# The input's sums of squares by accumulating DMAs, with more warm-up products and a later load of the gates' weights

## The chip, the cores and the metric

The kernel runs on one core of a Trainium2 chip. The metric is the device time of one execution in microseconds (us). Five engines work beside each other, each through its own instructions in order: TensorE (PE, matrix products; PEld is its load of the stationary operand), VectorE (DVE), ScalarE (ACT), GpSimd (POOL) and SyncE (SP, which only issues DMAs here). DMAs are issued by SyncE, ScalarE and GpSimd; those that add to what stands at their target are all issued by GpSimd.

## What is computed

One residual block of a streaming encoder on `x` of 512 tokens by 2048 channels, in float32. The part around the change is its beginning:

```python
hn = rmsnorm(h, norm_mix_g)          # y = x * rsqrt(mean(x*x) + EPS) * g
proj = hn @ w_in + b_in              # 2048 x 11272
(q, k, v, o_pre, i_pre, f_pre, cb, cc, ch, gm_pre, gc_pre) = jnp.split(proj, offs, axis=-1)
```

Behind it come the mLSTM, a short convolution, their merge through gates, `w_out` with the residual, and the feed-forward part with `w_up` and `w_down`, each with products of the same kind. The factor `rsqrt(mean(x*x) + EPS)` of a token is the same for all output channels, so the kernel multiplies by it (`rstd`) after the products.

## The kernel before

Everything is kept transposed: channels on the partitions, the 512 tokens along the free axis. Products of two 256-channel blocks with the tokens are done by a scheme with seven products in place of eight (`PRODUCTS` and `P1`), and each float32 product as three passes with a high and a low part (`three`, L280 to L282: high times high, high times low, low times high).

*Cells and items.* A pair of 128-channel blocks of the activations is a cell. The input has eight (0 to 7). An item is a pair of output blocks. Its weights come in four steps for the input phase; one step holds two half steps (`r` = 0, 1), each with one cell, of 21 products (`cell_mm`). Items 0 and 1 are interleaved in steps 0 to 7; from step 8 on (`START = 8`) each item has four steps in a row: item 2 has steps 8 to 11, item 3 steps 12 to 15. Steps `2q` and `2q + 1` of the first eight use cells `2q` and `2q + 1`.

*What a cell needs* (`x_task`): a load (cells 0 to 4 into `buf`, one of `mA`, `mB`, `z2`, `zs[0]`, `zs[1]`; cells 5 to 7 into a `raw` tile), a scaling by the norm's weight on ScalarE (`scaled`, L962), sums on VectorE (L343 to L353), a high part on ScalarE (`hi`, L357), a low part on VectorE (`lo`, L360), and a square on ScalarE (L952) for the sum over channels. For cells 0 to 4 the square follows `hi` and overwrites `buf`; for cells 5 to 7 it stands ahead of the scaling and goes from `raw` into `xbufs[c % 5]`, that is `mA`, `mB`, `z2`.

*What a step's weights need* (`weight_task`): a load into one of six `raw` tiles; sums on VectorE (L212 to L222); per half a high part on ScalarE (L232, four buffers) and a low part on VectorE (L236, three buffers). The load is SyncE's DMAs (L251 and L252 fill 128 KB each, L261 brings 512 KB), and GpSimd's two accumulating DMAs of 128 KB into the fills (L254). Steps 0, 1, 2 and 4 (`ALONE`) load 512 KB alone and do the first sum on VectorE.

*Sums of squares* (`sum_tokens`): eight products with `ones` per cell (L442) into bank `SIDE`, one output column each. In steps 0, 2, 4 and 6 one such group follows each half step. `rows_stages` makes `rstd` of it: `cols_a` (scale, square root), `cols_b` (reciprocal, correction, and L453, a diagonal of the result), `rows_pe` (L456, the product of `ones` with the diagonal) and `rows_post` (a copy to `rstd`).

*Order of the beginning.* `order` lists the tasks: cell 0, step 0's weights, cell 1, step 1's weights, and so on to cell 7, step 7's weights, then step 8's and on. The loop from L1242 on goes through it: in iteration `i` it emits the sums and high part of task `i + 1` (with the scaling of task `i + 2` between them), the low part of task `i`, the loads that have become possible (six tasks ahead of the last finished low part), and the half steps that have all their operands. Ahead of it come 18 warm-up products on zeros (L1195), `pcol`'s first part, the first loads, and the load of the gates' weights `gst` into `mC` on ScalarE's queue (L1207; eight of 264 columns of `w_v0`, so 32 bytes at a time).

Behind the loop stand `small_loads` (ten small DMAs on GpSimd), the weights of steps 8 and 9, and the main loop over the steps. A step `s` of it emits, in this order: VectorE's work for the weights of steps `s + 1` and `s + 2`, interleaved with the evacuations of items that ended (L310 to L313); `side_posts`; TensorE's two half steps; `gate_step`; one entry of `side`, whose first function is emitted at once, and whose second becomes a side post of the next step; and from step `START + hold` on the posts of ended items (L688, the multiplication by `rstd`, and more), of which items 0 and 1 have been waiting since step 8. So `cols_a` is emitted in step 8, `cols_b` and the product of `rows_pe` in step 9, `rows_post` in step 10.

*The gates.* `gate_weights`, in step 8, clears a `raw` tile on GpSimd (L478) and fills it from `gst` on ScalarE and VectorE (L482 to L485). `gate_mm` (L498 to L503) follows the half steps of step 9 (cells 0 to 2), step 10 (3 to 5) and step 11 (6 and 7); the result is copied from its bank in step 11.

Of the kernel before, what the change touches and what calls it, by code (L numbers as in the profile page):

```python
# [12 lines left out]
ALU = mybir.AluOpType  # L13

P = 128
T = 512
# [4 lines left out]
DV = 256  # L21
# [23 lines left out]
def kpair(c):  # L45

    q, r = divmod(c, 2)
    return 4 * q + r, 4 * q + 2 + r
# [23 lines left out]
def tile_block(ctx: ExitStack, tc: tile.TileContext, xT, w1, w_v0, w_v1, w_v2, w_bm, w_bc, w_out, w_up, w_down,  # L72
               par, b_if, b_v, outT):
    nc = tc.nc
    V, A, G, PE, SP = nc.vector, nc.scalar, nc.gpsimd, nc.tensor, nc.sync
# [14 lines left out]
    def f(ap):  # L90
        return ap.bitcast(F32)

    def C(shape, dt, s):
        return const.tile(shape, dt, tag=s, name=s)
# [15 lines left out]
    rstd = C([P, T], F32, "rstd")  # L110

    def col(base, j): return pcol[:, base + j:base + j + 1]
    def g_mix(j): return col(0, j)
# [9 lines left out]
    P_BANK, SIDE = bank[3], bank[7]  # L123
    SETS = (bank[0:3], bank[4:7])

    mA, mB, mC = C([P, 1280], F32, "mA"), C([P, 1032], F32, "mB"), C([P, T], F32, "mC")
    z2 = C([P, 2 * T], F32, "z2")
    zs = [C([P, 2 * T], F32, f"z{i}") for i in range(2)]
# [12 lines left out]
    side, posts, side_posts, late = deque(), deque(), [], []  # L141
# [275 lines left out]
    def rsqrt_a(src, scale, eps, n):  # L417

        v, y = sm("nv")[:, :n], sm("ny")[:, :n]
        if isinstance(eps, float):  # L420
            V.tensor_scalar(v, src, scale, eps, op0=ALU.mult, op1=ALU.add)
        else:
            V.scalar_tensor_tensor(v, src, scale, eps, op0=ALU.mult, op1=ALU.add)
        A.activation(y, v, AF.Sqrt)

    def rsqrt_b(dst, n):

        v, y, t = sm("nv")[:, :n], sm("ny")[:, :n], sm("nt")[:, :n]
        V.reciprocal(y, y)
        V.tensor_mul(t, y, y)  # L430
        V.tensor_mul(t, t, v)
        V.tensor_scalar(t, t, -0.5, 1.5, op0=ALU.mult, op1=ALU.add)
        V.tensor_mul(dst, y, t)
# [3 lines left out]
    def sum_tokens(ps, sq, n, nt, first, last):  # L437

        for b in range(n):
            for t in range(nt):  # L440
                o = (b * nt + t) * P
                PE.matmul(ps[:, t:t + 1], sq[:, o:o + P], ones[:, 0:1], start=first and b + t == 0,  # L442
                          stop=last and b == n - 1, skip_group_check=True)

    def rows_stages(ps, dst, diag, nt=4):

        def cols_a():
            rsqrt_a(ps[:, :nt], 1.0 / D, EPS, nt)

        def cols_b():  # L450
            rsqrt_b(rs1[:, :nt], nt)
            for t in range(nt):
                V.tensor_scalar(diag[:, t * P:(t + 1) * P], ident, rs1[:, t:t + 1], None, op0=ALU.mult)  # L453

        def rows_pe():
            PE.matmul(SIDE[:, :nt * P], ones, diag[:, :nt * P], start=True, stop=True)  # L456

        def rows_post():
            A.activation(dst[:, :nt * P], SIDE[:, :nt * P], AF.Copy)  # L459

        return cols_a, cols_b, rows_pe, rows_post
# [7 lines left out]
    gb = [mA[:, :T], mA[:, T:2 * T], mB[:, :T], mB[:, T:2 * T], mC, z2[:, :T], z2[:, T:]]  # L469

    gst = mC[:, :KD * 8].rearrange("p (k n) -> p k n", n=8)
# [455 lines left out]
            j1, j2 = kpair(p)  # L927
            x_items.append(Item(tiles_load(w1, c + j1, c + j2), 4, X, sig_post(d, c, j1, j2, s)))

    sqs = {}  # L930
    xbufs = [mA, mB, z2, zs[0], zs[1]]

    def x_task(c):

        k1, k2 = kpair(c)
        t = cell_task(X, c, xT)
        cell_load = t.load
        buf = xbufs[c % 5]

        def load():  # L940
            if c < 5:
                SP.dma_start(buf[:, :T], xT[k1])
                SP.dma_start(buf[:, T:2 * T], xT[k2])
            else:
                cell_load()

        def square(srcs):
            assert c < 5 or c - 5 not in sqs
            sqs[c] = buf
            for i, src in enumerate(srcs):  # L950
                w = src.shape[-1]
                A.activation(buf[:, i * w:(i + 1) * w], src, AF.Square)  # L952

        def scaled():
            if c < 5:
                t.new_raw()
                srcs = buf[:, :T], buf[:, T:2 * T]
            else:
                srcs = t.two()
                square(srcs)  # L960
            for ap, src, k in zip(t.two(), srcs, (k1, k2)):
                A.activation(ap, src, AF.Copy, scale=g_mix(k))  # L962

        cell_hi = t.hi

        def hi():
            cell_hi()
            if c < 5:
                square([buf[:, :2 * T]])

        t.load, t.pre, t.hi = load, scaled, hi
        return t
# [115 lines left out]
    order = [t for ts in tasks for t in ts]  # L1088
# [4 lines left out]
    def load_next():  # L1093
        i = n_load[0]
        while n_lo[0] < i and order[n_lo[0]].done:
            n_lo[0] += 1
        if i == len(order) or i - n_lo[0] + held[0] == RAW or (order[i].ready and not order[i].ready()):
            return False
        order[i].load()
        n_load[0] += 1  # L1100
        return True

    def loads():
        while load_next():
            pass
# [5 lines left out]
    def lo_ops(t):  # L1111

        def done():
            t.done = True

        if isinstance(t.wh, list):
            return [lambda: t.lo(0), lambda: (t.lo(1), done())]
        return [lambda: (t.lo(), done())]
# [73 lines left out]

    warm = actp.tile([P, T], F32R, tag="act", name="warm")
    G.memset(f(warm), 0.0)
    for _ in range(18):  # L1195
        PE.matmul(bank[6], warm[:, :P], warm, start=True, stop=True)
    del warm
    A.dma_start(pcol[:, :16], par[:, :16])
# [5 lines left out]
    for h in range(HEADS):  # L1204
        G.memset(mrow[32 * h:32 * h + 2], 1.0)
    loads()
    A.dma_start(gst, w_v0[:, :, DV:DV + 8])  # L1207

    def small_loads():
        G.dma_start(pcol[:, 16:], par[:, 16:])  # L1210
# [17 lines left out]
    def start_sums(t, ahead=None):  # L1228
        start_pre(t)
        for fn in t.sums:  # L1230
            fn()
        if ahead:
            start_pre(ahead)
        if isinstance(t.wh, list):
            t.hi(0)
            t.hi(1)
        else:
            t.hi()

    todo_mm = deque((s, r) for s in range(START) for r in range(2))  # L1240
    start_sums(order[0], order[1])
    for i in range(at[START]):  # L1242
        start_sums(order[i + 1], order[i + 2])
        for fn in lo_ops(order[i]):
            fn()
        loads()
        while todo_mm:
            s, r = todo_mm[0]
            it, q = steps[s]
            c = 2 * q + r  # L1250
            if i < at[s] or c not in X:
                break
            todo_mm.popleft()
            cell_mm(it, q, r, wt[s])
            if s % 2 == 0:
                sum_tokens(SIDE, sqs.pop(c), 2, 4, c == 0, c == 7)
            if q == 3 and r == 1:
                evac_first(it)
    assert not todo_mm
# [4 lines left out]
    loads()  # L1264
    ended = [steps[START - 2][0], steps[START - 1][0]]

    cols_a, cols_b, rows_pe, rows_post = rows_stages(SIDE, rstd, gb[5])
    side_posts.append(cols_a)
    side.append((noop, cols_b))
    side.append((rows_pe, rows_post))  # L1270

# [15 lines left out]

                side.append((noop, scaled))

    hold = 2  # L1290
    credit = 0.0
    urgent = {it.num for it in items_all if it.urgent}

# [9 lines left out]
    for s in range(START, len(steps)):  # L1303
# [90 lines left out]
        if s >= START + hold:  # L1394
            credit = min(credit, 2.5)
            rush = not main or any(x[0] in urgent for x in posts)
            for x in list(posts)[:2]:
                cost, fn = x[1][0]
# [12 lines left out]
        if not main and it.n == 11:  # L1411
            plain_rows = bank[3]
            cols_a, cols_b, _, _ = rows_stages(LCOLS[0], None, mC, 2)
# [17 lines left out]
    cols_a, cols_b, _, _ = rows_stages(LCOLS[1], None, mC, 2)  # L1431
# [64 lines left out]
```

## Time and profile before

| | us |
|---|---|
| median of 3 runs | 2630.27 |
| lowest and highest | 2627.07 and 2635.22 |
| the profiled execution | 2635.24 |
| span of its instructions | 2633.5 |

The span is the time from the first to the last instruction of the profiled execution. A row of the timeline has the start in us from the span's start, the duration in us, the engine (with q for its queue: an instruction that only issues or waits), the line, the operation, out<-in, the shapes where it has any, and the number of instructions of that kind in the row; in brackets the idle time of the engine ahead of it, and what ended it. In the table of stretches each row is a window, with each engine's busy us and, in parentheses, its instructions, then the granted clock of TensorE as a share of the full one, the mean busy share of the 16 DMA engines, and GB/s. That share can pass 1, since packets overlap. In the waits a row names who waited for what, the sum in us, how often, and the longest. A DMA queue's row has packets, MB, and the time of its packets as a share of 16 engines' span. A row of DMA issues ends with the median time from issue to landing.

### The profile page before, as it was taken

The numbers are of one execution on the slowest core, as the hardware profiler recorded it, in microseconds if no ns is written. First come the engines' busy times: TensorE is split into PE (matmuls) and PEld (weight loads), VectorE is DVE, ScalarE is ACT, GpSimd is POOL, SyncE is SP. The second block draws the span as 40 slices with busy tenths as digits, with TensorE's granted clock in tenths as the row PEclk, the third lists the DMA queues.
The fourth block names the chain that finished last, engine by engine and source line by source line (L and its number), as shares of the span: only waits on it lengthen the run. The fifth ranks groups of instructions, "written<-read, shape, count | busy, mean of one in ns | idle before, by whom it ended". The sixth has DMA issues, their size and how long they took to land.

```text
span 2633.5 us, 55501 instructions
## 1 busy us (share of the span) xinstructions
PE 2579.5 (98%) x21146; PEld 2562.4 (97%) x21146; DVE 2112.6 (80%) x3308; ACT 1291.9 (49%) x1748; POOL 799.5 (30%) x922
## 2 busy tenths in 40 slices
PE   8999999999999999999899999999999999999997
PEld 8999999999999999999899999999999999999997
DVE  8577778886777888877989888888888897677756
ACT  7444554546556543435545544454444454444433
POOL 2443333333333211222333333333333323232310
PEclk8999999999999999999999999999999999999998
DMA  8799989898898897787898988988888889898976
GB/s 214 179 225 232 240 218 260 219 253 222 228 252 220 233 296 222 222 241 211 230 223 225 225 221 222 221 227 221 221 223 223 214 227 229 212 239 207 237 173 193
DMA packets 462557, 592.55 MB, mean 225 GB/s; under 512 B 42784, under 2 KB 296736, under 8 KB 462288
## 3 DMA queue, kind: packets, MB, share of 16 engines
q1 hardware_dynamic: 301968, 419.79, 50.8%
q0 software_dynamic: 133088, 124.04, 31.7%
q10 hardware_dynamic: 27232, 45.17, 4.7%
q8 instruction: 165, 2.70, 0.4%
q14 instruction: 104, 0.85, 0.1%
HBM read 531.17 MB, written 57.67 MB: 224 GB/s over the span
## 4 chain that ended last, share of the span: by engine, by line
PE 70%; DVE 4%; issue 1%; DMA 1%; ACT 0%; SPq 0%; DVEq 0%; POOL 0%; ACTq 0%; POOLq 0%
PE bank L282 22%; PE bank L280 22%; PE bank L281 22%; DVE wl L236 1%; DVE act L360 1%; DMA raw<-in_w_up_dram 1%; PE bank L1170 0%; PE bank L442 0%; PE bank L1171 0%; PE bank L1172 0%; PE bank L639 0%; DVE z L311 0%; DVE raw L217 0%; DVE z L310 0%; DVE xraw L343 0%
## 5 line engine op out<-in xcount | busy, mean ns | idle before, releaser
L280 PE MATMUL bank<-act,wh 128*128 128x256 f32 x6760 | 1929.3, 285 | 11.8 <-ACT wh L232 5.9
L282 PE MATMUL bank<-act,wl 128*128 128x256 f32 x6760 | 1920.5, 284 | 20.1 <-DVE wl L236 16.7
L281 PE MATMUL bank<-act,wh 128*128 128x256 f32 x6760 | 1917.9, 284 | 0.0
L282 PEld LDWEIGHTS bank<-act,wl 128*128 128x128 f32 x6760 | 1302.7, 193 | 24.0 <-DVE wl L236 19.9
L280 PEld LDWEIGHTS bank<-act,wh 128*128 128x128 f32 x6760 | 1302.8, 193 | 16.1 <-ACT wh L232 6.3
L232 ACT ACTIVATE wh<-raw 128x896 fp32r<-128x896 f32 x856 | 812.8, 953 | 1030.1 <-PE bank L281 700.6
L281 PEld LDWEIGHTS bank<-act,wh 128*128 128x128 f32 x6760 | 1302.9, 193 | 2.8 <-issue 1.7
L236 DVE TENSOR_TENSOR wl<-raw,wh 128x896 fp32r<-128x896 f32 x856 | 930.3, 1088 | 343.8 <-PE bank L282 232.9
L254 POOL DMA_DIRECT2D raw<-in_w_up_dram x344 | 298.9, 953 | 597.5 <-DMA raw<-in_w_up_dram 309.7
L254 POOL DMA_DIRECT2D raw<-in_w_dram x280 | 243.8, 945 | 519.2 <-DMA raw<-in_w_dram 338.3
L217 DVE TENSOR_TENSOR raw<-raw 128x256 f32<-128x256 f32 x428 | 179.9, 420 | 10.9 <-DMA raw<-in_w_down_dram 6.2
L254 POOL DMA_DIRECT2D raw<-in_w_down_dram x112 | 99.9, 1006 | 264.5 <-DMA raw<-in_w_down_dram 142.1
L222 DVE TENSOR_TENSOR raw<-raw 128x256 f32<-128x256 f32 x428 | 179.6, 420 | 0.3
L310 DVE TENSOR_TENSOR z<-bank,z 128x512 f32<-128x512 f32 x131 | 89.9, 687 | 34.7 <-ACT z L304 23.1
L357 ACT ACTIVATE act<-xraw 128x1792 fp32r<-128x1792 f32 (+1 forms) x52 | 85.6, 1647 | 55.8 <-DVE xraw L353 46.5
L185 ACT ACTIVATE wh<-raw 128x256 fp32r<-128x256 f32 x96 | 40.1, 417 | 136.9 <-PE bank L281 116.4
L360 DVE TENSOR_TENSOR act<-xraw,act 128x1792 fp32r<-128x1792 f32 (+1 forms) x52 | 101.8, 1958 | 0.0
L688 DVE TENSOR_TENSOR z<-z,rstd 128x1024 f32<-128x1024 f32 x83 | 101.1, 1219 | 0.2 <-ACT rstd L459 0.2
L190 DVE TENSOR_TENSOR wl<-raw,wh 128x256 fp32r<-128x256 f32 x96 | 40.5, 422 | 71.7 <-PE bank L282 41.2
L311 DVE TENSOR_TENSOR z<-bank,z 128x512 f32<-128x512 f32 x131 | 89.8, 686 | 1.7
L313 DVE TENSOR_TENSOR z<-bank,z 128x512 f32<-128x512 f32 x131 | 89.6, 684 | 0.0
L254 POOL DMA_DIRECT2D raw<-in_w_out_dram x48 | 41.8, 968 | 128.0 <-DMA raw<-in_w_out_dram 91.9
(214 smaller groups left out, 1389.5 us busy)
## 6 DMA issues: line engine op xcount, KB each, us to landing
raw<-in_w_up_dram SPq DMA_DIRECT2D x172, 512.0 KB, 5.6
raw<-in_w_dram SPq DMA_DIRECT2D x144, 512.0 KB, 5.9
raw<-in_w_up_dram SPq DMA_DIRECT2D x344, 128.0 KB, 4.0
raw<-in_w_up_dram POOLq DMA_DIRECT2D x344, 128.0 KB, 5.4
raw<-in_w_down_dram SPq DMA_DIRECT2D x80, 512.0 KB, 5.6
raw<-in_w_dram SPq DMA_DIRECT2D x280, 128.0 KB, 4.3
raw<-in_w_dram POOLq DMA_DIRECT2D x280, 128.0 KB, 5.3
raw<-in_w_out_dram SPq DMA_DIRECT2D x32, 512.0 KB, 4.8
```

Source lines behind the costliest of these rows:

```text
L217: V.tensor_add(x[:, 6], x[:, 5], x[:, 0])
L222: V.tensor_add(x[:, 2], x[:, 6], x[:, 1])
L232: A.activation(seven(t.wh[r]), half(r), AF.Copy)
L236: V.tensor_sub(seven(t.wl[r]), half(r), seven(f(t.wh[r])))
L254: G.dma_start(at(i), a21, accum_op=ALU.add)
L280: PE.matmul(ps, h, xh, start=start, stop=False, skip_group_check=True)
L281: PE.matmul(ps, h, xl, start=False, stop=False, skip_group_check=True)
L282: PE.matmul(ps, l, xh, start=False, stop=stop, skip_group_check=True)
L310: return [lambda: V.tensor_add(z[:, 0:4:3], b0, two(z[:, 1])), lambda: V.tensor_add(z[:, 1:3], b1, two(z[:, 3])), lambda: V.tensor_add(z[: ...
L311: lambda: V.tensor_add(z[:, 1:3], b1, two(z[:, 3])),
L360: V.tensor_sub(t.act[:, NW:NW + m], t.raw[:, :m], f(t.act[:, :m]))
L688: V.tensor_mul(sb_pair(it.z), sb_pair(it.z), two(rstd))
```

## The change

- The squares of cells 1 to 7 are added into `mA`, which holds cell 0's, by seven accumulating DMAs of 512 KB on GpSimd. They are emitted one iteration after the square, at the iteration's end behind its loads. Cell 5 squares into `mB`, cell 6 into `z2`, cell 7 into `mB` again.
- The eight groups of `sum_tokens` in the first eight steps go; one group over `mA` is emitted in step 10 as an entry of `side`, behind two empty ones. `cols_a` is emitted in step 11, `cols_b` and the product of `rows_pe` in step 12, `rows_post` in step 13. The diagonal goes into `mB` in place of `z2`.
- The squares of cells 0 to 4 are emitted behind the high parts of the weights that follow the cell, in place of ahead of them.
- 40 warm-up products in place of 18.
- The gates' weights load in iteration 6 of the loop, still on ScalarE's queue.
- `hold` is 5 in place of 2: the posts begin in step 13.

```diff
-    sqs = {}
-    xbufs = [mA, mB, z2, zs[0], zs[1]]
+    xbufs = [mA, mB, z2, zs[0], zs[1], mB, z2, mB]
+    squares, sums_of_squares = [], []
...
-        buf = xbufs[c % 5]
+        buf = xbufs[c]
...
         def square(srcs):
-            assert c < 5 or c - 5 not in sqs
-            sqs[c] = buf
             for i, src in enumerate(srcs):
                 w = src.shape[-1]
                 A.activation(buf[:, i * w:(i + 1) * w], src, AF.Square)
+            if c:
+                sums_of_squares.append(lambda: G.dma_start(mA[:, :2 * T], buf[:, :2 * T], accum_op=ALU.add))
...
         def hi():
             cell_hi()
             if c < 5:
-                square([buf[:, :2 * T]])
+                squares.append(lambda: square([buf[:, :2 * T]]))
...
-    for _ in range(18):
+    for _ in range(40):
         PE.matmul(bank[6], warm[:, :P], warm, start=True, stop=True)
...
     loads()
-    A.dma_start(gst, w_v0[:, :, DV:DV + 8])
...
     for i in range(at[START]):
+        todo = sums_of_squares[:]
+        sums_of_squares[:] = []
+        if i == 6:
+            A.dma_start(gst, w_v0[:, :, DV:DV + 8])
         start_sums(order[i + 1], order[i + 2])
+        if isinstance(order[i + 1].wh, list):
+            for fn in squares:
+                fn()
+            squares[:] = []
         for fn in lo_ops(order[i]):
             fn()
         loads()
+        for fn in todo:
+            fn()
...
             cell_mm(it, q, r, wt[s])
-            if s % 2 == 0:
-                sum_tokens(SIDE, sqs.pop(c), 2, 4, c == 0, c == 7)
...
-    cols_a, cols_b, rows_pe, rows_post = rows_stages(SIDE, rstd, gb[5])
-    side_posts.append(cols_a)
+    for fn in sums_of_squares:
+        fn()
+    assert not squares
+    cols_a, cols_b, rows_pe, rows_post = rows_stages(SIDE, rstd, mB[:, :T])
+    side.append((noop, noop))
+    side.append((noop, noop))
+    side.append((lambda: sum_tokens(SIDE, mA, 2, 4, True, True), cols_a))
     side.append((noop, cols_b))
     side.append((rows_pe, rows_post))
...
-    hold = 2
+    hold = 5
```

## The prediction

> **What bounds the kernel now.** I read the page first, then the busy time by stretches, then the timeline of each engine through the first 120 us, which is all that the change touches.
>
> ```profile
> span 2633.5 us, 55501 instructions
> ...
> PE 2579.5 (98%) x21146; PEld 2562.4 (97%) x21146; DVE 2112.6 (80%) x3308; ACT 1291.9 (49%) x1748; POOL 799.5 (30%) x922
> ...
> q0 software_dynamic: 133088, 124.04, 31.7%
> ```
>
> TensorE is busy for 98% of the span, so a gain must take work off it or close one of its gaps. The head is different:
>
> ```profile
> 10.00:20.00 10.00, 5.75 (x26) 5.46 (x26) 9.83 (x13) 9.33 (x11) 1.17 (x2) 0.55 0.80 245
> 20.00:30.00 10.00, 10.00 (x56) 10.00 (x57) 8.75 (x13) 7.53 (x8) 0.97 (x2) 0.60 0.66 187
> 30.00:40.00 10.00, 10.00 (x87) 10.00 (x86) 7.72 (x10) 6.10 (x7) 1.59 (x2) 1.00 0.49 127
> 40.00:50.00 10.00, 10.00 (x87) 10.00 (x86) 9.54 (x13) 9.61 (x14) 1.75 (x2) 1.00 0.85 197
> 70.00:80.00 10.00, 9.02 (x72) 8.62 (x73) 5.42 (x9) 2.75 (x4) 6.77 (x10) 1.00 1.07 261
> 185.00:190.00 5.00, 2.29 (x14) 2.09 (x13) 4.97 (x10) 2.77 (x4) 2.39 (x2) 0.85 0.79 162
> 190.00:195.00 5.00, 5.00 (x38) 5.00 (x37) 3.92 (x10) 2.95 (x5) 1.25 (x2) 0.81 0.82 270
> ```
>
> From 10 to 20 us VectorE is full (9.83 of 10) while TensorE is busy for 5.75 at a granted clock of 0.55. Behind the five engines stand the granted clock, the DMA share and GB/s: the DMA engines are half idle at 30 to 40 us and full (1.07) at 70 to 80. Two engines, then, can take over as the bound once TensorE has less to do.
>
> ```profile
> 15.05 0.58 PE L282 MATMUL bank<-act,wl 128*128 128x256 f32 x1 [1.26 <-DVE wl L236]
> 36.95 1.84 PE L442 MATMUL bank<-ones,z 128*128 128x1 f32 x16
> 38.65 0.36 PE L280 MATMUL bank<-act,wh 128*128 128x256 f32 x1
> 75.29 0.28 PE L280 MATMUL bank<-act,wh 128*128 128x256 f32 x1
> 86.74 0.28 PE L282 MATMUL bank<-act,wl 128*128 128x256 f32 x1
> 88.59 0.93 PE L498 MATMUL bank<-act,gw 128*128 128x512 f32 x3 [1.57 <-issue]
> 113.64 0.28 PE L280 MATMUL bank<-act,wh 128*128 128x256 f32 x1
> 118.67 0.28 PE L280 MATMUL bank<-act,wh 128*128 128x256 f32 x1
> ```
>
> These are TensorE's milestones: step 8 starts at 75.29, step 9 ends at 86.86, the gates' products start at 88.59 after a gap, step 12 runs from 113.64 to 118.67. A step is 5.03 us, a half step 2.52.
>
> **Off TensorE at the head.** One cell's sums of squares take 1.70 us of it (36.95 to 38.65), eight cells 13.6 us and more at the low clock. What that is worth is set by VectorE, whose work is unchanged:
>
> ```profile
> 8.93 0.69 DVE L212 TENSOR_TENSOR raw<-raw 128x512 f32<-128x512 f32 x1 [0.79 <-DMA raw<-in_w_dram]
> ...
> 32.18 1.09 DVE L236 TENSOR_TENSOR wl<-raw,wh 128x896 fp32r<-128x896 f32 x1 [3.23 <-PE bank L282]
> ...
> 45.79 1.09 DVE L236 TENSOR_TENSOR wl<-raw,wh 128x896 fp32r<-128x896 f32 x1 [0.29 <-PE bank L282]
> ...
> 55.79 0.68 DVE L343 TENSOR_TENSOR xraw<-xraw 128x512 f32<-128x512 f32 x1
> ...
> 59.42 1.09 DVE L236 TENSOR_TENSOR wl<-raw,wh 128x896 fp32r<-128x896 f32 x1 [1.02 <-PE bank L282]
> ...
> 61.22 2.02 DVE L360 TENSOR_TENSOR act<-xraw,act 128x1792 fp32r<-128x1792 f32 x1
> 63.95 2.08 DVE L236 TENSOR_TENSOR wl<-raw,wh 128x896 fp32r<-128x896 f32 x2
> ```
>
> Up to cell 7's low part (ending at 61.22 + 2.02 = 63.24) VectorE waited for TensorE 3.23 + 0.29 + 1.02 = 4.54 us, and 0.79 for the first weights. Without both, cell 7 is ready at 57.9; three half steps then remain (the second of step 6 and both of step 7), so step 8 could start at 57.9 + 7.6 = 65.5, which is 9.8 us earlier. That is all the head can give. The clock adds nothing beyond it, since VectorE sets the pace. The 40 warm-up products cost nothing:
>
> ```profile
> 1.38 5.71 PE L1196 MATMUL bank<-warm 128*128 128x512 f32 x18 [1.38 <-POOL warm L1194]
> ...
> SPq L261 <- DMA mC<-in_w_v_dram: 5.9, 1, 5.9
> ```
>
> Forty at 5.71/18 = 0.317 us end by 14.1, and the third real product can't run before the first low part (15.05 - 0.79 = 14.26); if that cover were gone the price is 1 us. The gates' weights leave the head, where SyncE's queue waited 5.9 us for them; VectorE's 0.79 is the most that this brings. At iteration 6 they have 40 us until they are read and cost nothing. Squares behind the high parts take 1.04 us out of ScalarE's way, inside the same bound.
>
> **The new wait.** Cell 7 now squares into mB, which cell 5's accumulating DMA must have read. That DMA is queued on GpSimd behind the accumulating loads of step 7's weights. Nearest rows:
>
> ```profile
> 46.91 0.33 SPq L251 DMA_DIRECT2D raw<-in_w_dram  x1
> 50.23 1.75 POOL L254 DMA_DIRECT2D raw<-in_w_dram  x2 [5.97 <-DVE xraw L343]
> 53.17 1.14 ACT L952 ACTIVATE z<-xraw 128x512 f32<-128x512 f32 x2
> DMA to landing us min/median/max: 6.0/9.3/14.3
> ...
> raw<-in_w_dram POOLq DMA_DIRECT2D x280, 128.0 KB, 5.3
> ```
>
> The rows are, in order, SyncE's issue of step 7's first fill, GpSimd's accumulation into that fill, ScalarE's square of cell 7 (both halves), the landing times of line 156's accumulating DMA into h_d (512 KB), and the median of the 128 KB accumulations into raw. Step 7's fills go out when step 4's low part ends (46.88). GpSimd issues their accumulation from 50.23 to 51.98, and cell 5's sum comes next in its queue, if cell 3's has landed by then. No accumulation of 512 KB into SBUF is in this trace. The nearest by size is h_d's, 6.0 us at least and 9.3 in the middle; the nearest by target is raw's, a quarter of the size, 5.3. So the sum lands at 57.3 to 61.3 on before's time, where ScalarE squared cell 7 at 53.17. Behind that square on ScalarE wait cell 7's scaling and step 6's high parts. VectorE's start on cell 7, at 55.79 with 0.25 us of slack behind the scaling, slips by 3.9 to 7.9 us. I take a landing of 7.0, near the shorter rows because the target is SBUF as raw is, hence 5.5. Step 8 then starts 9.8 - 5.5 = 4.3 us earlier, at 71.0, and step 9 ends at 82.6.
>
> The Trainium skill's DMA: Bandwidth & Descriptors (Anatomy of one DMA) prices a GpSimd-issued DMA at about 2.0 us plus its bytes over 436 GB/s: 3.2 us here, an estimate, by which the whole sum would be some 3 us and not 6. The trace disagrees where it can be asked: h_d's 512 KB never took less than 6.0.
>
> **The gates.** Their weights are built after a memset on GpSimd that stands behind step 13's accumulations, ten small loads and step 14's:
>
> ```profile
> 66.07 0.33 SPq L251 DMA_DIRECT2D raw<-in_w_dram  x1
> ...
> 74.95 1.75 POOL L254 DMA_DIRECT2D raw<-in_w_dram  x2 [2.15 <-DMA raw<-in_w_dram]
> ...
> 85.60 0.64 POOL L478 MEMSET gw<- 128x640 f32 x1
> ```
>
> Step 13's fills go out when step 7's second low part ends (63.95 + 2.08 = 66.03). With 5.33 us taken out of VectorE's queue and 5.5 put in, that end doesn't move. GpSimd's chain from 74.95 to the products at 88.59 is 13.6 us. Fills that took 8.9 us to reach GpSimd under a full DMA could take 3.3, as at 46.91: 5.6 us sooner. Against that, seven sums of 0.524 MB at queue 0's price (31.7% of 2633.5 us for 124.04 MB, 6.73 us per MB) are 24.7 us of all 16 engines, and the idle share from 10 to 50 us (0.20, 0.34, 0.51, 0.15) is 12 us: up to 12.7 us later. I take no movement, so the 4.3 us are lost here, and TensorE waits 88.6 - 82.6 = 6.0 us instead of 1.73. After a gap of that kind the clock falls: the rows at 185 to 195 show 0.15 x 5 + 0.19 x 5 = 1.7 us lost after one. That is added.
>
> **Given back later.** The one remaining sum, 1.70 us, now lies in step 10, on the path. The rows of rstd come out of step 12 instead of step 9:
>
> ```profile
> 118.44 1.08 DVE L236 TENSOR_TENSOR wl<-raw,wh 128x896 fp32r<-128x896 f32 x1
> ...
> 91.32 0.17 DVE L429 RECIPROCAL ny<-ny 128x4 f32<-128x4 f32 x1
> ...
> 92.33 0.88 DVE L453 TENSOR_SCALAR z<-identw,rs 128x128 f32<-128x128 f32 x4
> ...
> 93.95 1.02 PE L456 MATMUL bank<-z,ones 128*128 128x512 f32 x2
> ...
> 98.87 2.36 DVE L688 TENSOR_TENSOR z<-z,rstd 128x1024 f32<-128x1024 f32 x2 [0.19 <-ACT rstd L459]
> ```
>
> In step 12 VectorE has item 2's evacuation, then step 13's low parts until 119.52, and only then the diagonal (91.32 to 93.21, 1.89 us): 121.4. TensorE, whose next instruction after step 12 is that product, is there at 118.67 and waits 2.7 us. Before, the same product (L456 at 93.95) stood behind the gates' and met no wait. hold = 5 starts the normalizing of items 0 to 2 three steps later, on a VectorE that is busy for 5.42 of 10 us at 70 to 80: 0, and 1.2 us, one such operation, if it falls before a low part.
>
> **Sum.** Head and gates 0, clock +1.7, sum in step 10 +1.7, rows +2.7: +6.1 on 2635.24 (span 2633.5 and 1.7 around it), 2641.3. The profiled execution is 5 us above the median of 2630.27, so I forecast 2636.3 for the median. A measurement here tells some 0.3%, 7.9 us, from no change.
>
> **Rivals.**
> - *The head's gain survives (faster).* For: ScalarE has idle stretches and DMA is half empty at 30 to 40 us. If the sums land before cell 7 needs mB, step 7's low part ends 5.3 earlier (60.7), the fills reach GpSimd at 64.0, the gates start at 77.6, when step 9 ends at 77.1, and the clock holds: -11.0 + 1.7 + 2.7 = -6.6, 2623.7; with the rows hidden too, -9.3, 2621.0. Against: the order on GpSimd. 0.14, of which 0.10 passes 0.3%.
> - *DMA is over its capacity (slower).* Step 13's fills land late, GpSimd's chain starts late, the gates with it: up to 12.7, with half of it 6.4, 2642.7. It decides once GpSimd takes step 13's fills some 2 us after 74.95. For: share 1.07 at 70 to 80 us already. Against: the engines idled before. 0.32.
> - *Short sums.* If a sum lands in the 3.3 us that step 7's fills took to reach GpSimd (46.91 to 50.23), it is there at 55.3 and delays cell 7 by 1.9; step 7's low part is 3.4 earlier, the gates too: -3.4 + 6.1 = +2.7, 2633.0. For: nothing but the size of the fills. Against: h_d's 6.0. 0.20. The skill's price above would put it here.
>
> The same page of the Trainium skill (Rules for kernel authors) has an accumulate wait for the semaphore of an earlier one on the same bytes, which speaks against this change: the seven sums would go one by one and hold GpSimd's queue. No run shown yet has two on the same bytes; it favours the second rival.
>
> **Numbers.** Forecast 0.34. Slower by over 0.3%: 0.32. Faster: 0.10. Within: 0.34 + 0.20 + 0.04 = 0.58. The range runs from the first rival's edge to past the second's, 2624 to 2645.
>
> **What would show it.** Step 8 near 71; ScalarE's square of cell 7 waiting for a DMA; the gates' products near 88.6 behind 6 us of gap and a half clock; 2.7 us before L456. Wrong, if step 8 starts at 66 and the gates before 80, or if step 8 starts after 75.

## The result, and the profile after

The kernel with the change takes 2647.97 us (median of 6 runs, 2647.05 to 2652.51), the kernel before on the same chip 2630.60. The ratio is 1.0074, with a 95% interval of 1.0061 to 1.0086: slower by 0.74%; the two medians differ by 17.4 us. The forecast was 2636.3 in a range of 2624 to 2645. The profiled execution took 2647.36.

From the page of the kernel after, the lines that answer to the first three of before:

```profile
span 2645.6 us, 55338 instructions
...
PE 2573.9 (97%) x21056; PEld 2553.5 (97%) x21056; DVE 2111.0 (80%) x3308; ACT 1292.2 (49%) x1748; POOL 806.0 (30%) x929
...
q0 software_dynamic: 134096, 127.71, 32.4%
```

TensorE has 90 instructions and 5.6 us of work fewer, and the span is 12.1 us longer. The 1008 packets and 3.67 MB that queue 0 gained are the seven sums. The table of stretches of the kernel after (columns as before, the last three are granted clock, DMA share and GB/s):

```profile
30.00:40.00 10.00, 8.89 (x72) 8.48 (x71) 9.83 (x13) 9.66 (x13) 2.11 (x3) 1.00 1.00 214
40.00:50.00 10.00, 7.40 (x59) 7.20 (x60) 9.83 (x15) 7.55 (x9) 2.78 (x5) 1.00 1.04 249
50.00:60.00 10.00, 2.95 (x25) 2.75 (x23) 1.46 (x1) 0.02 (x1) 1.68 (x2) 0.87 1.03 264
60.00:70.00 10.00, 5.74 (x25) 5.45 (x26) 7.48 (x11) 7.53 (x9) 7.06 (x8) 0.50 0.94 180
70.00:80.00 10.00, 9.57 (x73) 9.10 (x72) 7.77 (x12) 4.36 (x6) 4.33 (x5) 0.95 1.08 237
80.00:90.00 10.00, 8.99 (x73) 8.68 (x72) 4.18 (x7) 0.95 (x1) 5.54 (x9) 1.00 1.04 261
90.00:100.00 10.00, 3.23 (x12) 2.97 (x13) 3.92 (x10) 4.71 (x15) 4.11 (x7) 0.58 0.20 28
```

Before, the DMA engines were half empty at 30 to 40 us (0.49). Now they are full from 30 to 90. From 30 to 50 VectorE has no idle time left (9.83 of 10), as the forecast had it. From 50 to 60 VectorE works for 1.46 us, ScalarE for 0.02 and TensorE for 2.95: nearly everything stands still while the DMAs run. The timeline of TensorE shows the milestones of the kernel after (starts of steps 8, 9, 10, 11, 12, 13 and 14, with the gates' products and L456 between):

```profile
77.84 0.35 PE L280 MATMUL bank<-act,wh 128*128 128x256 f32 x1
84.42 0.28 PE L280 MATMUL bank<-act,wh 128*128 128x256 f32 x1
96.77 1.62 PE L498 MATMUL bank<-act,gw 128*128 128x512 f32 x3 [7.15 <-issue]
104.42 0.27 PE L280 MATMUL bank<-act,wh 128*128 128x256 f32 x1
116.39 0.36 PE L280 MATMUL bank<-act,wh 128*128 128x256 f32 x1
125.02 0.28 PE L280 MATMUL bank<-act,wh 128*128 128x256 f32 x1
132.74 2.08 PE L456 MATMUL bank<-mB,ones 128*128 128x512 f32 x2 [2.53 <-DVE mB L453]
133.83 1.20 PE L280 MATMUL bank<-act,wh 128*128 128x256 f32 x1
140.21 0.28 PE L280 MATMUL bank<-act,wh 128*128 128x256 f32 x1
```

Against before, step 8 starts 2.6 us later (77.84 for 75.29), step 10 is 10.0 later (104.42 for 94.41), step 12 is 11.4 (125.02 for 113.64) and step 14 is 16.5 (140.21 for 123.71). Up to step 160 the distance stays near 16 (920.7 for 905.2); behind that the two executions differ by single windows of half clock, which brings the spans to 12.1. So the loss has three places: the end of the head, the gates, and steps 12 and 13. The three waits of TensorE that go with them, from the table of waits:

```profile
PE bank L280 <- ACT wh L232: 10.3, 1, 10.3
PE bank L498 <- issue: 7.2, 1, 7.2
...
PE bank L456 <- DVE mB L453: 2.5, 1, 2.5
```

Behind the first stand these rows of the timelines of ScalarE, VectorE and GpSimd (L950 is the square, L952 the sum, L254 the accumulation of a weight):

```profile
59.98 1.15 ACT L950 ACTIVATE mB<-xraw 128x512 f32<-128x512 f32 x2 [11.46 <-DMA mA<-mB]
...
62.39 0.69 DVE L343 TENSOR_TENSOR xraw<-xraw 128x512 f32<-128x512 f32 x1 [10.93 <-ACT xraw L962]
...
50.12 1.56 POOL L952 DMA_DIRECT2D mA<-mB  x1
60.50 0.86 POOL L952 DMA_DIRECT2D mA<-z  x1 [8.82 <-DMA raw<-in_w_dram]
61.03 3.88 POOL L254 DMA_DIRECT2D raw<-in_w_dram  x4
```

Cell 5's sum, issued at 50.12, lands at 59.96. ScalarE waits 11.46 us for it before it may overwrite mB with cell 7's square, and VectorE waits 10.93 us behind ScalarE. On GpSimd the next sum, cell 4's, may not start before cell 5's has landed either, and four accumulations of weights stand behind it until 61.03. (The bracket of that row names a load of weights. That the earlier sum held it is read from the times: it goes out 0.54 us after cell 5's landing, as it does in the second experiment, 60.00 after 59.46, and in the ninth, 55.33 after 54.79.)

### The profile page after: what moved, and what is told of

Its sections match the earlier page's. It is cut to its first block, busy times and chain, and to the rows that moved or that the text cites. A ratio compares the mean times of both kernels' runs of the same rounds, so it can differ in the third digit from the quotient of the medians.

```text
span 2645.6 us, 55338 instructions
## 1 busy us (share of the span) xinstructions
PE 2573.9 (97%) x21056; PEld 2553.5 (97%) x21056; DVE 2111.0 (80%) x3308; ACT 1292.2 (49%) x1748; POOL 806.0 (30%) x929
## 4 chain that ended last, share of the span: by engine, by line
PE 79%; DVE 5%; DMA 2%; issue 2%; ACT 0%; SPq 0%; DVEq 0%; POOL 0%; POOLq 0%; ACTq 0%
PE bank L282 25%; PE bank L280 25%; PE bank L281 25%; DVE act L360 1%; DVE wl L236 1%; PE bank L639 1%; DMA h_d<-z 1%; DMA raw<-in_w_up_dram 1%; PE bank L442 0%; PE bank L1170 0%; PE bank L1171 0%; PE bank L1172 0%; DMA raw<-in_w_dram 0%; DVE xraw L343 0%; DVE z L311 0%
## 5 line engine op out<-in xcount | busy, mean ns | idle before, releaser
L280 PE MATMUL bank<-act,wh 128*128 128x256 f32 x6760 | 1929.1, 285 | 16.1 <-ACT wh L232 10.3
L254 POOL DMA_DIRECT2D raw<-in_w_up_dram x344 | 299.1, 962 | 595.0 <-DMA raw<-in_w_up_dram 285.0
L254 POOL DMA_DIRECT2D raw<-in_w_dram x280 | 244.6, 966 | 507.3 <-DMA raw<-in_w_dram 310.0
L254 POOL DMA_DIRECT2D raw<-in_w_down_dram x112 | 99.7, 993 | 266.0 <-DMA raw<-in_w_down_dram 150.9
L310 DVE TENSOR_TENSOR z<-bank,z 128x512 f32<-128x512 f32 x131 | 89.8, 685 | 39.4 <-ACT z L304 26.8
L313 DVE TENSOR_TENSOR z<-bank,z 128x512 f32<-128x512 f32 x131 | 89.5, 683 | 0.0
L254 POOL DMA_DIRECT2D raw<-in_w_out_dram x48 | 41.7, 965 | 128.4 <-DMA raw<-in_w_out_dram 75.5
```

Source lines behind the costliest of these rows:

```text
L254: G.dma_start(at(i), a21, accum_op=ALU.add)
L280: PE.matmul(ps, h, xh, start=start, stop=False, skip_group_check=True)
L310: return [lambda: V.tensor_add(z[:, 0:4:3], b0, two(z[:, 1])), lambda: V.tensor_add(z[:, 1:3], b1, two(z[:, 3])), lambda: V.tensor_add(z[: ...
```

## Experiments

All kernels of a group ran on one chip beside runs of the kernel before; the ratios are to those, whose medians were 2626.43 (experiments 1 to 4), 2628.09 (5 to 8) and 2627.88 (9 to 12). The starts of steps are from each kernel's one profiled execution.

| kernel | step 8 | step 10 | median | ratio, 95% interval |
|---|---|---|---|---|
| before, first trace | 75.3 | 94.4 | 2630.60 | |
| before, second trace (5) | 71.5 | 89.2 | 2627.11, one run | |
| after | 77.8 | 104.4 | 2647.97 | 1.0074, 1.0061 to 1.0086 |
| 1 no sums | 68.4 | 88.1 | 2631.56 | 1.0011, 1.0003 to 1.0020 |
| 2 cell 7 in another buffer | 78.2 | 102.4 | 2646.17 | 1.0068, 1.0056 to 1.0080 |
| 3 clearing on VectorE | 79.1 | 96.3 | 2640.23 | 1.0046, 1.0033 to 1.0059 |
| 4 before and three edits | 69.2 | 88.1 | 2625.24 | 0.9992, 0.9983 to 1.0000 |
| 6 bytes without the order | 77.4 | 101.8 | 2647.69 | 1.0074, 1.0060 to 1.0088 |
| 7 no sums, rows early | 68.6 | 89.9 | 2627.52 | 0.9995, 0.9986 to 1.0005 |
| 8 three edits and clearing | 70.3 | 87.6 | 2623.14 | 0.9983, 0.9974 to 0.9991 |
| 9 small sums | 72.7 | 90.8 | 2636.44 | 1.0022, 1.0011 to 1.0033 |
| 10 changed, mended | 80.4 | 98.5 | 2635.54 | 1.0028, 1.0017 to 1.0038 |
| 11 warm-ups only | 69.4 | 89.0 | 2625.38 | 0.9993, 0.9984 to 1.0002 |
| 12 gates' load only | 71.7 | 89.5 | 2626.11 | 0.9996, 0.9987 to 1.0005 |

**1. Without the sums.** The changed kernel with

```diff
-            if c:
-                sums_of_squares.append(lambda: G.dma_start(mA[:, :2 * T], buf[:, :2 * T], accum_op=ALU.add))
```

> The changed kernel without its seven accumulating DMAs (left out: rstd comes from cell 0's squares alone). Theory: the loss is made at the head by what these DMAs do to the queues: ScalarE waits 11.46 us for cell 5's sum before it squares cell 7 into mB, and GpSimd reaches the gates' memset 8.2 us later than before (93.79 against 85.60). Without them ScalarE's square of cell 7 waits for no DMA, step 8 starts at 65.5 to 67, the memset is done by 85 and the gates' products start at 76 to 86. The sum in step 10 (+1.7) and the wait ahead of L456 (+2.5) stay. Sum against the kernel before: between -8 and 0, ratio 0.997 to 1.000, some 20 us below the changed kernel. Rival (the other edits make the loss: warm-ups, hold, rows moved to step 12, gates' weights later): the time stays within 5 us of the changed kernel, 2643 to 2653.

Measured: 2631.56, ratio 1.0011, step 8 at 68.4. The rival is out: the seven DMAs make 0.63% of the changed kernel's 0.74%. But step 8 and the ratio both miss what the theory expected, on the slow side: without its DMAs the change is still no gain. Rows of the timelines of VectorE, TensorE and GpSimd:

```profile
67.22 0.42 DVE L217 TENSOR_TENSOR raw<-raw 128x256 f32<-128x256 f32 x1 [2.99 <-DMA raw<-in_w_dram]
...
68.39 0.55 PE L280 MATMUL bank<-act,wh 128*128 128x256 f32 x1 [2.93 <-DVE z L310]
...
79.76 0.64 POOL L478 MEMSET gw<- 128x640 f32 x1
```

and two of its stretches:

```profile
60.00:70.00 10.00, 7.07 (x53) 6.89 (x52) 6.11 (x11) 3.13 (x4) 4.11 (x5) 0.89 1.13 288
70.00:80.00 10.00, 10.00 (x79) 9.74 (x77) 4.74 (x7) 0.95 (x1) 8.60 (x15) 0.94 0.52 129
```

Step 7 starts at 60.3, 9.9 us earlier than in the first trace of before; at step 8 only 6.9 are left. VectorE waits 2.99 us for the DMA of step 10's weights, and the evacuation (L310) for which TensorE waits stands behind that in its queue. The DMA engines are at 1.13 there. They are free from 70 to 80 (0.52), where the changed kernel's are full until 90. The gates' tile is cleared at 79.76, 14.0 us before the changed kernel's (93.79, below).

**2. Another buffer for cell 7.** The changed kernel with

```diff
-    xbufs = [mA, mB, z2, zs[0], zs[1], mB, z2, mB]
+    xbufs = [mA, mB, z2, zs[0], zs[1], mB, z2, zs[0]]
...
-                it.z = (zs[0], zs[1], z2)[it.num] if it.num < 3 else zs[(it.num + 1) % 2]
+                it.z = (mB[:, :2 * T], zs[1], z2)[it.num] if it.num < 3 else zs[(it.num + 1) % 2]
...
-    cols_a, cols_b, rows_pe, rows_post = rows_stages(SIDE, rstd, mB[:, :T])
+    cols_a, cols_b, rows_pe, rows_post = rows_stages(SIDE, rstd, zs[0][:, :T])
```

> The changed kernel with cell 7 squaring into zs[0], whose sum (cell 3's) landed at 48.28, instead of mB, whose sum (cell 5's) landed at 59.96; items 0's output goes into mB and the diagonal into zs[0]. All seven DMAs stay. Theory: the wait of 11.46 us on ScalarE goes, step 8 starts at 67 to 70 instead of 77.8, TensorE keeps its clock at 57 to 71; but the queue of GpSimd stays as long, the memset at 88 to 94, so the gates' products start at 91 to 97 behind a longer gap than 7.2 us, and most of the gain is lost there: 2640 to 2648, up to 8 us below the changed kernel. Rival (DMA engines over capacity, 24.7 us of added packets): step 8 stays after 75, since its weights or step 7's come late whatever the buffer; no change of the time.

Measured: 2646.17, step 8 at 78.2. The wait of ScalarE is gone, and nothing is won that the intervals could tell. The time fits both expectations; step 8, after 75, is the rival's and not the theory's. Rows of the timelines of GpSimd and VectorE:

```profile
60.00 0.86 POOL L952 DMA_DIRECT2D mA<-z  x1 [8.23 <-ACT wh L232]
60.53 3.88 POOL L254 DMA_DIRECT2D raw<-in_w_dram  x4
...
69.78 0.43 DVE L217 TENSOR_TENSOR raw<-raw 128x256 f32<-128x256 f32 x1 [10.49 <-DMA raw<-in_w_dram]
```

VectorE now stands still for 10.49 us a little further on in its queue, at the sums of step 8's weights, and step 7's low parts, for which TensorE waits, stand behind them. The fills of those weights had landed by 50.9; GpSimd issued their accumulation at 60.53, behind cell 4's sum, which had waited for cell 5's, and it landed at 69.7. Two causes were left: the order on GpSimd, or full DMA engines. (The next expectation calls these weights step 7's and takes the landing, 53.7, of the fills that follow.)

**6. The bytes without the order.** The second experiment with

```diff
-                sums_of_squares.append(lambda: G.dma_start(mA[:, :2 * T], buf[:, :2 * T], accum_op=ALU.add))
+                sums_of_squares.append(lambda: G.dma_start(h_d[2 * c:2 * c + 2].rearrange("j p t -> p j t"), sb_pair(buf), accum_op=ALU.add))
```

> The second experiment (cell 7 in zs[0]) with the seven DMAs of 512 KB kept as accumulating ones, but each into a part of h_d of its own, so that none waits for the one before it (left out: the sum over the cells, rstd comes from cell 0 alone). Theory: what holds step 8 back there is the order on GpSimd (cell 4's sum waits for cell 5's to land, 8.23 us, and step 7's weights' accumulations stand behind it); without that wait the accumulation of the fills that landed at 53.7 goes out near 54 and not at 60.53, and step 8 starts at 68.4 to 72 instead of 78.2: 2632 to 2640. Rival (the bytes themselves: 24.7 us of all DMA engines): the weights land late even when issued in time, step 8 stays after 75, the time within 4 us of the second experiment's 2646.2.

Measured: 2647.69, step 8 at 77.4. The rival holds. From the timelines of GpSimd and VectorE:

```profile
53.42 1.79 POOL L254 DMA_DIRECT2D raw<-in_w_dram  x2 [0.58 <-DMA raw<-in_w_dram]
56.68 0.86 POOL L254 DMA_DIRECT2D raw<-in_w_dram  x1 [1.47 <-DMA raw<-in_w_dram]
58.20 0.86 POOL L254 DMA_DIRECT2D raw<-in_w_dram  x1 [0.66 <-DMA raw<-in_w_dram]
...
66.41 0.43 DVE L217 TENSOR_TENSOR raw<-raw 128x256 f32<-128x256 f32 x1 [6.76 <-DMA raw<-in_w_dram]
...
91.37 0.64 POOL L478 MEMSET gw<- 128x640 f32 x1
```

and from its stretches:

```profile
60.00:70.00 10.00, 4.25 (x29) 4.05 (x29) 3.52 (x6) 2.17 (x3) 2.94 (x4) 0.74 1.14 256
70.00:80.00 10.00, 7.15 (x47) 6.77 (x45) 5.97 (x10) 2.17 (x3) 3.87 (x4) 0.84 1.14 256
```

The accumulations for step 8 go out at 53.42, 7 us earlier than in the second experiment, and still land only at 65.3 and 66.4: they take 12 us each, with the engines at 1.14. The gates' tile is cleared at 91.37, with the others that carry the bytes and not with the first experiment's 79.76. Two reserves. The target is DRAM here and SBUF there; the sums' own packets (1792 of 2 KB here, 896 of 4 KB there) take 21.4 us of all engines here and 20.0 in the second. And the wait on GpSimd is gone, but not the order in its DMA queue. Of the DMAs from 56 to 62 us:

```profile
q0 software_dynamic: 441, 0.86, 77.4%
...
raw<-in_w_dram SPq DMA_DIRECT2D x4, 128.0 KB, 13.2
```

Queue 0 is GpSimd's. Its 441 packets carry 0.86 MB, so nearly all are the sums' packets of 2 KB, and none to speak of the weights' of 1 KB. The two sums issued at 50.03 and 50.75 land first, at 60.2 and 64.1, and step 8's accumulations, though issued at 53.42, land behind them. But SyncE's fills, which have a queue of their own, are late in that stretch too: 13.2 us to land, against 7.1 in the same stretch of the first experiment. So the bytes delay the weights in both ways, by full engines and by standing ahead in queue 0, and no run here tells the two shares apart.

**9. The order with few bytes.** The second experiment with

```diff
-                sums_of_squares.append(lambda: G.dma_start(mA[:, :2 * T], buf[:, :2 * T], accum_op=ALU.add))
+                sums_of_squares.append(lambda: G.dma_start(mA[:, :64], buf[:, :64], accum_op=ALU.add))
```

> The second experiment (cell 7 in zs[0]) with its seven accumulating DMAs still one behind the other on the same bytes of mA, but of 64 columns (32 KB) instead of 1024 (512 KB) (left out: the rest of each sum). With the sixth experiment it makes a square: there the bytes without the order, here the order with a sixteenth of the bytes. Theory as it now stands (the DMA engines are full from 40 us on, so the bytes decide): step 8 within 2 us of the first experiment's 68.4, the time 2629 to 2635, within 0.15% of the first experiment's ratio of 1.0011. Rival (the sums hold GpSimd's queue, since each waits for the landing of the one before it, and the weights' accumulations stand behind): step 8 after 73, the time 2637 to 2646.

Measured: 2636.44, ratio 1.0022, step 8 at 72.7: between the two expectations. From the timelines of GpSimd and TensorE:

```profile
55.33 0.86 POOL L952 DMA_DIRECT2D mA<-z  x1 [5.71 <-ACT act L357]
55.86 3.89 POOL L254 DMA_DIRECT2D raw<-in_w_dram  x4
...
72.74 0.28 PE L280 MATMUL bank<-act,wh 128*128 128x256 f32 x1
```

The four accumulations stand behind a sum here too, until 55.86. With this all four corners of the square have been run. Step 8, against 68.4 without sums: the order alone 4.3 us later, the bytes alone (into DRAM) 9.0, both 9.8. In the whole time: order 0.0011 (2.9 us), bytes 0.0063 (16.6), both 0.0057 (15.0), each difference uncertain by some 0.0015. The bytes are enough for the loss, and the order adds nothing to them that can be told; alone it is worth a few us.

**3. Clearing on VectorE.** The changed kernel with

```diff
-        G.memset(f(gwt[:, :640]), 0.0)
+        V.memset(f(gwt[:, :640]), 0.0)
```

> The changed kernel with the clearing of the gates' tile on VectorE instead of GpSimd, so that it no longer stands behind GpSimd's accumulations and small loads. Theory: the gates' products start right behind step 9, at 89.5 to 90.5 instead of 96.77, without the 7.15 us gap and with the full clock: -7 to -11, 2637 to 2641, unless step 10's own weights, which GpSimd accumulates at 77.6 and 78.7, or step 13's are late in turn. Rival (the lateness is in the DMA engines, not in the order on GpSimd): the gap moves to step 10 or 11, and the time stays within 3 us of the changed kernel.

Measured: 2640.23, ratio 1.0046. Against the changed kernel's row

```profile
93.79 0.64 POOL L478 MEMSET gw<- 128x640 f32 x1
```

the same clearing stands on VectorE 6 us earlier, and TensorE's first product of the gates follows step 9 without a gap:

```profile
87.44 0.59 DVE L478 MEMSET gw<- 128x640 f32 x1
...
91.04 0.86 PE L498 MATMUL bank<-act,gw 128*128 128x512 f32 x3
```

From step 9 to step 10 it takes 10.3 us in place of 20.0. The ratio falls by 0.0028, 7.4 us: the gates' term, as expected, and the rival is out. Behind it TensorE has the known wait ahead of L456, 2.7 us here, and one of 0.7.

**7. Rows early.** The first experiment with

```diff
-    side.append((noop, noop))
-    side.append((noop, noop))
...
-    hold = 5
+    hold = 3
```

> The first experiment (no DMAs of the sums; rstd from cell 0 alone) with the one sum on TensorE in step 8 instead of step 10, the diagonal and its product in step 10 instead of 12, and hold 3 instead of 5. In the first experiment steps 10 to 17 took 50.8 us and in the kernel before 44.4. Theory: these 6.4 us are the moved sum (1.7), the wait ahead of L456 (2.5) and what follows both; with the rows two steps earlier VectorE builds the diagonal ahead of a free TensorE, the sum stays on the path: 2 to 5 us below the first experiment's 2631.6, 2626.5 to 2629.5. Rival (it is hold and the posts, or the order of VectorE's work whatever the step): within 1 us of 2631.6.

Measured: 2627.52, 0.0016 (4.2 us) below the first experiment, as the theory had it. From step 10 to step 17 it takes 44.9 us (89.9 to 134.8) where it took 50.8; from step 8 to step 10, where the sum now lies, it takes 21.3 in place of 19.7. The rows and hold were moved together, so their shares are not told apart.

**4, 11, 12 and 8. The other edits on the kernel before.** The fourth experiment is the kernel before with 40 warm-ups, the gates' load in iteration 6 and the squares of cells 0 to 4 behind the high parts; the 11th and 12th have the first or the second of these alone; the 8th has the three and the clearing on VectorE.

```diff
-    for _ in range(18):
+    for _ in range(40):
...
-    A.dma_start(gst, w_v0[:, :, DV:DV + 8])
...
+        if i == 6:
+            A.dma_start(gst, w_v0[:, :, DV:DV + 8])
...
-                square([buf[:, :2 * T]])
+                squares.append(lambda: square([buf[:, :2 * T]]))
```

> The kernel before with the other edits of the head alone: 40 warm-up products, the gates' weights loaded in iteration 6, squares of cells 0 to 4 behind the weights' high parts. Sums of squares stay on TensorE, hold stays 2, rows stay in step 9. Theory: VectorE still waits for TensorE in part (4.54 us before), so step 8 starts 2 to 6 us earlier than 75.29; GpSimd's chain of the gates moves with step 7's low part or not at all, so -4 to 0 against the kernel before. Rival (these edits are the whole 8.8 us that the changed kernel was ahead in step 5): -8 or more. Second rival (they give nothing, the head's gain comes from taking the sums off TensorE): 0 within 1 us, step 8 within 1 us of 75.29.

> The kernel before with 40 warm-up products and nothing else. Theory: VectorE sets the pace of the head, but in the kernel before TensorE at half clock (11.03 to 28.09 in one trace, 12.96 to 19.79 in the second) set it for the first step; more warm-ups keep the clock and save 1 to 2 us: 2624 to 2627, ratio 0.9993 to 0.9998. Rival (price without gain, since the products end at 14.1 us): 0 to +1 us.

> The kernel before with the gates' weights loaded in iteration 6 and nothing else. Theory: SyncE's queue no longer waits 5.9 us behind that load, so that the third step's weights come earlier, but VectorE had only 0.79 us of waiting there: 0 to -1 us. Rival (it makes the whole of the fourth experiment's gain): -1 to -3 us, ratio 0.9990 or below.

> The fourth experiment (the kernel before with 40 warm-ups, later gates' weights, squares behind the high parts) with the clearing of the gates' tile on VectorE. Theory: its trace shows one gap of 1.4 us ahead of the gates' products, which this closes: 1 to 2 us below 2625.2, ratio to the kernel before 0.9985 to 0.9990. Rival (another wait takes its place, or the clearing delays VectorE's low parts): within 0.5 us of 2625.2 or above.

Measured: 0.9992, 0.9993, 0.9996 and 0.9983, in this order; the last is a little better than expected. The single edits gain too little to tell from nothing; the three together are at the edge of their interval. With the clearing on VectorE the gain is 0.17% (4.5 us), the only version here whose interval lies wholly on the faster side. So it beats both kernels. It keeps the sums on TensorE. The 11th's stretches show what the warm-ups do:

```profile
10.00:20.00 10.00, 8.95 (x61) 7.96 (x60) 9.68 (x12) 9.23 (x11) 1.55 (x2) 1.00 0.77 253
20.00:30.00 10.00, 10.00 (x87) 10.00 (x86) 9.79 (x15) 7.86 (x8) 1.46 (x3) 1.00 0.75 213
```

The granted clock is 1.00 where the first trace of before had 0.55 and 0.60.

**5. The kernel before once more.**

> The kernel before, unchanged, for a second trace of its head. Its profiled execution (2635.24) lay 5 us above its median, with the clock halved from 11.03 to 28.09. Theory: that half clock is a matter of where the 3.4 us windows of the clock fall, and in an execution near the median the clock drops less in the first 30 us, so that step 8 starts 3 to 6 us earlier than 75.29 and the time is 2624 to 2629. Rival: the head is the same in every execution (step 8 within 1 us of 75.3) and the 5 us lie later, in half-clock stretches behind step 20.

Measured: 2627.11, step 8 at 71.5, as the theory had it:

```profile
10.00:20.00 10.00, 5.74 (x27) 5.44 (x27) 9.83 (x13) 9.22 (x11) 1.87 (x2) 0.66 0.88 273
20.00:30.00 10.00, 10.00 (x87) 10.00 (x87) 9.79 (x15) 7.53 (x8) 0.81 (x3) 1.00 0.69 196
```

The half clock ends at 19.8 us here and at 28.1 in the first trace. Step 8 is 3.8 us earlier, and all of it is there by step 1, which starts at 25.5 in place of 29.3. The Trainium skill's TensorE: Matmul & The Clock Gate (What's actually happening) has the clock set by free-running windows of some 3.4 us, so that the same kernel gets a different number of slow products in each run; the two traces agree.

**10. The changed kernel, mended.** The second and third experiments together, with one empty entry less and

```diff
-    hold = 5
+    hold = 4
```

> The changed kernel with cell 7 in zs[0], the gates' tile cleared on VectorE, and the sum and rows one step earlier (one empty entry instead of two, hold 4 instead of 5); all seven DMAs of 512 KB stay and all is computed. Theory: the parts add up: 0 for the buffer, -8 for the clearing (third experiment), -2 to -4 for the rows, so 2634 to 2638, ratio 1.002 to 1.004; what is left above the kernel before is step 8, held back by the bytes. Rival (the three are one wait seen three times): no better than the third experiment, 2639 to 2642.

Measured: 2635.54, ratio 1.0028, as the theory had it: the parts add up. Behind step 8, which is still at 80.4, TensorE has no wait for the gates or the rows left. What remains is step 8, ahead of which VectorE waits 10.39 us for an accumulation of step 8's weights, as in the second experiment (10.49). That this is the bytes is argued from the square: no run takes the sums out of this kernel.

## Why the prediction was wrong

*The step that failed* is the effect of the sums' bytes, which was put at nothing, and with it the choice of the forecast over the second rival. At the gates' fills the bytes were weighed (24.7 us against 12 us of idle share) and then set to zero: "I take no movement", between bounds of 5.6 us sooner and 12.7 us later. For step 8's weights, which come through the same engines, they were not weighed at all; only the buffer's wait was. The runs put 9.0 us of step 8 and some 12 us of the gates' clearing (91.37 for 79.76) on the bytes alone. The rival's own test, that GpSimd takes step 13's fills some 2 us after 74.95, was passed by 9 us (83.96); its sign of a wrong forecast, step 8 after 75, came too; and the clearing behind them came 8.2 us after the first trace's 85.60. The size given for the bytes was near: in the trace of the kernel after, the sums' own packets (896 of 4 KB in queue 0) take 20.7 us of all engines where the forecast had 24.7. Queue 0 as a whole, from 20 to 110 us, in the kernel after and without sums:

```profile
q0 software_dynamic: 4606, 6.87, 45.9%
...
q0 software_dynamic: 4398, 3.58, 26.0%
```

That is 17.9 us more. The share of all queues together rises by 11.5 us only (summed by ten-us stretches, 7.62 for 6.47), since the kernel after, which is behind by then, moves 1.4 MB less of SyncE's loads in that stretch. What failed was the idle share that was to swallow the bytes: it was no reserve. Without any sum the faster head takes its weights earlier and fills the engines itself from 40 to 70 us (0.95, 1.11 and 1.13), and four of the seven sums go out after 50 us.

*The head's 9.8.* VectorE's part was right: without sums, cell 7's low part ends at 57.7 (forecast 57.9), and step 7 starts 9.9 us earlier than in the trace used. Two things were missed. The weights' DMAs take over as the bound by step 8, so 6.9 are left. And that trace had an unlucky clock; against the second trace of before the first experiment gains 3.1 at step 8, and warm-ups alone, with TensorE still making the sums, 2.1. "The clock adds nothing" was wrong: the 4.54 us that VectorE waited for TensorE were, by the later traces, the half clock's. In the second trace of before they are 2.8, and in the 11th experiment, with the clock full and the sums still on TensorE, VectorE waits for TensorE nowhere before 66 us. So taking the sums off TensorE is worth nothing that can be told: the seventh and fourth experiments differ by 0.0003, with some 0.0013 of uncertainty.

*The new wait* was put in the right place and sized at 5.5 us (bounds 3.9 to 7.9); VectorE waited 10.93. The landing taken at 7.0 was 9.8. Yet this did not decide step 8 (71.0 forecast, 77.84 measured): without the wait, in the second experiment, it is 78.2.

*The rest of the sum.* The gap ahead of the gates was 7.15 for 6.0. The clock term, 1.7, shows as 7.65 us for the gates' products and what lies up to step 10 (96.77 to 104.42) in place of 5.82 (88.59 to 94.41): 1.8. The sum in step 10 cost 1.3 for 1.7 (steps 10 to 11, 11.97 for 10.68). The rows waited 2.53 for 2.7, but steps 12 and 13 grew by 5.1 (15.19 for 10.07): the product itself, in step 9 before, now lies there, and a stretch of half clock follows that wait, which the forecast had priced behind the gates' gap and not here. Two short stretches of the kernel after show it (clock 1.00, then 0.57):

```profile
128.00:132.00 4.00, 2.22 (x19) 2.01 (x17) 3.83 (x10) 1.57 (x2) 2.42 (x2) 1.00 0.70 178
132.00:136.00 4.00, 3.26 (x9) 2.22 (x10) 2.36 (x7) 0.00 (x0) 0.92 (x1) 0.57 1.11 218
```

The seventh experiment, which keeps the one sum on the path but moves it, the rows and hold to earlier steps, wins back 4.2 of these 6.4 us. Warm-ups and the gates' load at nothing stand: alone, each lies within its interval of no change.

Along the first traces the terms are 2.6 (forecast -4.3), 7.4 (forecast 6.0), 1.3 (1.7) and 5.1 (2.7): 16.4 where the sum said 6.1. Of the 10.3 us between, 6.9 are the head. By the ratios, the changed kernel's 1.0074 is made of 0.9992 (three edits), +0.0003 (sums off TensorE), +0.0016 (late sum, rows and hold), +0.0057 (the seven DMAs in another buffer) and +0.0006 (the wait for mB). Of the four additions only 0.0016 and 0.0057 are larger than their uncertainty, some 0.0013 to 0.0017.

## What to carry to other kernels

Half-empty DMA engines in the trace of before are no reserve for new bytes if the same change makes a faster head ask for its loads earlier: count the new bytes against the share in the stretches where the faster kernel will load, and look which loads will stand behind them in the same queue. When one wait is removed and the time stays, look in the same microseconds for the wait that was hidden under it; a square of four kernels (with and without the bytes, with and without the order) shows which alone is enough. And one trace of before can have an unlucky clock: a gain that is read off a half-clock stretch should be checked against a second execution.

## What the hardware showed that I had not expected

Accumulating DMAs of 512 KB from SBUF into SBUF took 5.0 to 10.8 us from issue to landing beside the weights' loads; the medians on the page of the kernel after:

```profile
mA<-z POOLq DMA_DIRECT2D x4, 512.0 KB, 7.1
...
mA<-mB POOLq DMA_DIRECT2D x3, 512.0 KB, 9.8
```

The Trainium skill's DMA: Bandwidth & Descriptors (Anatomy of one DMA) would give an estimate of 3.2 us; no run here came near it, the shortest being 5.0. Its rule that an accumulate waits for an earlier one on the same bytes (Rules for kernel authors) shows as GpSimd's 8.82 us ahead of the sum at 60.50, and costs 4.3 us at step 8 with a sixteenth of the bytes. In engine time the seven sums took 20.7 us of all engines for 3.67 MB, 5.6 us per MB, a little less than queue 0's average of 6.73.

The load of the gates' weights, 32 bytes at a time, took 10.3 us from issue to landing at the start of the kernel before, beside the first loads, and 4.6 us in iteration 6.
